# Down product of a conv-FFN: tokens in the partitions, 512 weight columns at a time

## The chip, the cores and the metric

One core of a Trainium2 chip runs the whole layer as one program. The metric is the device time of one execution in microseconds; before the change it is the median of 3 runs.

## What is computed

One layer of a hybrid backbone over 256 latent tokens with 2048 channels. The change lies in its last step, the gated MLP with its residual. Cut to that:

```python
def conv_ffn(h, w_up, conv_w, conv_b, w_down):
    u = h @ w_up
...
    gate, val = jnp.split(u, 2, axis=-1)
    return (jax.nn.silu(gate) * val) @ w_down
...
    x_new = x + g1 * mix_l
    h2_l = modulate(rms_norm(x_new, norm2_w), sh2, sc2)
    x_new = x_new + g2 * conv_ffn(h2_l, w_up, conv_w, conv_b, w_down)
```

`w_down` is 5632 x 2048 in float32, `g2` is one factor per channel (2048 of them), and the first `x_new`, called `x1` in the kernel, is added at the end.

## The kernel before

All activations stand with channels in the 128 partitions and tokens in the free dimension: `x1` is 16 tiles of 128 channels x 256 tokens, the gated MLP's inner values are 44 tiles `g[j]` of 128 x 2 x 256. Products are made in float32r from split operands: a value is a rounded high part and the remaining low part, and a product is high x high, low x high and high x low. In `g`, index 1 of the middle dimension is the high part of the activations and 0 the low part.

Weights come by SyncE's queue (SP) through `fetch` (L225, L227) into four buffers `wraw` of 128 x 1024 (512 KB each). `split` (L201) makes of 512 columns a high part `whi` on ScalarE (ACT, a cast, L206) and a low part `wlo` by a subtraction (L213) on VectorE (DVE), or, if `splits[1]` is not 0, every so many times on GpSimd (POOL). `whi` and `wlo` have four buffers each, so a cast waits until TensorE (PE) has done with the `whi` of four casts before.

The MLP's up stage (L1236 to L1246) works a tile of 128 gate and one of 128 value columns at a time, in two of the four `acc` banks of PSUM. `added` (L272) takes a bank out: a copy on ACT (L273), then an addition on DVE (L274). Convolution and SiLU follow on ACT and DVE (L1211 to L1222), and the result is split into `g[j]` (L231, L232). Between these, the vector of modulation factors is made up: DVE takes products of `w_ada` rows with the conditioning row `cb` (L338, one for each 128 x 1024 block that `araw` holds); `ada_done(48)` at L1247 finishes the last 16 columns of `adav`, which are `g2` (columns 48 to 63) by channel.

The down stage (L1248 to L1254) loops over the 16 tiles `c` of 128 output channels. For each, `col_tile` (L238) streams the 44 weight tiles of 128 x 128: the weights are loaded into the array, and `g` streams past. The high weights take 512 columns (both parts of 256 tokens, L262), the low weights 256 (L264), so a tile is 44 pairs. Then two DVE operations (L1252, L1253) add both halves of the bank, scaled by `adav`, to `x1[c]`, and ACT issues a store of 128 x 256 (L1254). The output leaves transposed and is turned on the host side.

What sets the order: PE's instructions of the stage are tied in the order of the code by `chain`. On the other engines a list scheduler orders the instructions by its own estimate of times, and each engine then executes its list strictly in that order; a waiting instruction holds all behind it. DMAs wait on the queue of the engine that issues them. The framework gives every DMA of SP and ACT one of eight semaphores in turn, in the order of its list (DMAHW0 to DMAHW7 in the rows below); a DMA waits until the earlier DMA on its semaphore has landed, unless that is known already.

## Time and profile before

| | us |
|---|---|
| median of 3 runs | 1700.16 (1699.24 to 1700.27) |
| profiled execution | 1700.9 |
| its span | 1699.1 |
| down stage, first to last start of its matmuls | 1450.0 to 1695.1 |
| PE busy in the span | 1680.0 |
| DVE, ACT busy in the span | 1241.0, 980.0 |

The page and the views show one execution, the profiled one; its own time is 1.8 us longer than its span. Busy time of an engine counts no waiting, no register and no DMA-issuing instructions. Matmuls are pipelined: a row of the timeline can say that a matmul lasts 0.39 us while the next starts 0.23 us later, so PE's pace is read from the starts. A row of a group gives line, engine, operation, output<-inputs, shape and count, then busy us and mean ns of one, then the idle time just ahead of it and what ended that. ACTq and SPq are the queues of ACT and SP in which DMAs are issued.

### The profile page before, as it was taken

Reading aid. Unit: us, or ns where it says so; the run is one execution under the profiler, and the core shown is the slowest. Engines: PE = TensorE matmul, PEld = TensorE weight load, DVE = VectorE, ACT = ScalarE, POOL = GpSimd, SP = SyncE. Lnnn points to the kernel's source line nnn. Section 1 sums busy time; section 2 is a strip of 40 time slices with the busy share of each in tenths; the row PEclk is TensorE's granted clock in tenths of the full one; section 3 lists DMA queues with packets and bytes.
Section 4 is the critical chain, followed back from the end, with each engine's and each line's share of the span. In section 5 each row is a group of like instructions: output and inputs, shape, how many; then the busy total and the mean of one; then the engine's idle time right before and its main releaser. Section 6 shows DMA issues by size and latency. Waiting matters only on the chain.

```text
span 1699.1 us, 29122 instructions
## 1 busy us (share of the span) xinstructions
PE 1680.0 (99%) x10460; PEld 1461.7 (86%) x10460; DVE 1241.0 (73%) x2375; ACT 980.0 (58%) x1984; POOL 310.9 (18%) x331
## 2 busy tenths in 40 slices
PE   7999999999999999999999999999999999999999
PEld 5779999998787888888888998888888888888887
DVE  5556765867688888788988797787878787644443
ACT  5324554756355777666766686666666666444443
POOL 0000213131210000001323200222222222222222
PEclk9999999999999999999999999999999999999999
DMA  9995532434566555688777566676767676666664
GB/s 384 402 408 194 165 127 90 140 109 155 181 200 233 172 188 186 203 280 279 267 260 261 181 200 217 217 238 224 237 227 237 222 241 223 199 203 193 199 201 135
DMA packets 108451, 368.75 MB, mean 217 GB/s; under 512 B 12176, under 2 KB 17040, under 8 KB 108304
## 3 DMA queue, kind: packets, MB, share of 16 engines
q1 hardware_dynamic: 103264, 362.51, 64.0%
q10 hardware_dynamic: 5040, 4.37, 0.8%
q8 instruction: 82, 1.34, 0.3%
q14 instruction: 65, 0.53, 0.1%
HBM read 364.73 MB, written 2.10 MB: 216 GB/s over the span
## 4 chain that ended last, share of the span: by engine, by line
PE 91%; DMA 4%; DVE 3%; ACT 1%; issue 1%; POOL 0%; SPq 0%; DVEq 0%; ACTq 0%
PE down L262 9%; PE upg L262 9%; PE upv L262 9%; PE gate L262 7%; PE down L264 5%; PE upg L264 5%; PE sweep L350 5%; PE upv L264 4%; PE gate L264 4%; PE mix L262 4%; PE mix L264 2%; PE pgb L262 2%; PE ab L350 2%; PE pga L262 2%; DMA ada<-in_w_ad 2%; PE dk L313 2%
## 5 line engine op out<-in xcount | busy, mean ns | idle before, releaser
L206 ACT CAST whi<-wraw 128x512 fp32r<-128x512 f32 (+2 forms) x1004 | 606.5, 608 | 397.3 <-PE down L262 110.5
L213 DVE TENSOR_TENSOR wlo<-wraw,whi 128x512 fp32r<-128x512 f32 (+2 forms) x888 | 608.6, 694 | 251.9 <-ACT whi L206 242.1
L213 POOL TENSOR_TENSOR wlo<-wraw,whi 128x512 fp32r<-128x512 f32 x116 | 157.0, 1353 | 576.4 <-ACT whi L206 555.5
L262 PE MATMUL down<-g,whi 128*128 128x512 f32 x704 | 243.6, 392 | 0.0
L262 PE MATMUL upg<-a,whi 128*128 128x512 f32 x656 | 229.0, 391 | 0.0
L262 PE MATMUL upv<-a,whi 128*128 128x512 f32 x656 | 229.0, 391 | 0.0
L264 PE MATMUL down<-g,wlo 128*128 128x256 f32 x704 | 195.4, 280 | 0.7 <-DVE wlo L213 0.7
L264 PE MATMUL upv<-a,wlo 128*128 128x256 f32 x656 | 182.8, 280 | 0.0
L264 PE MATMUL upg<-a,wlo 128*128 128x256 f32 x656 | 182.6, 280 | 0.0
L262 PE MATMUL gate<-a,whi 128*128 128x512 f32 x512 | 180.5, 398 | 0.7 <-ACT whi L206 0.7
L338 DVE CUSTOM_DVE_ANT_0 araw<-araw,cb 128x1024 f32<-128x1024 f32 x128 | 159.5, 1248 | 11.4 <-DMA araw<-in_w_ada 11.3
L262 PEld LDWEIGHTS down<-g,whi 128*128 128x128 f32 x704 | 131.0, 187 | 28.3
L262 PEld LDWEIGHTS upv<-a,whi 128*128 128x128 f32 x656 | 122.4, 187 | 26.6
L262 PEld LDWEIGHTS upg<-a,whi 128*128 128x128 f32 x656 | 122.4, 187 | 26.5
L264 PE MATMUL gate<-a,wlo 128*128 128x256 f32 x512 | 140.4, 284 | 0.0
L264 PEld LDWEIGHTS down<-g,wlo 128*128 128x128 f32 x704 | 132.9, 189 | 1.9 <-DVE wlo L213 1.0
L264 PEld LDWEIGHTS upv<-a,wlo 128*128 128x128 f32 x656 | 123.9, 189 | 0.5
L264 PEld LDWEIGHTS upg<-a,wlo 128*128 128x128 f32 x656 | 123.9, 189 | 0.5
L262 PEld LDWEIGHTS gate<-a,whi 128*128 128x128 f32 x512 | 94.4, 188 | 20.5 <-ACT whi L206 1.0
L264 PEld LDWEIGHTS gate<-a,wlo 128*128 128x128 f32 x512 | 96.5, 189 | 6.2 <-issue 1.8
L262 PE MATMUL mix<-a,whi 128*128 128x512 f32 x256 | 88.8, 396 | 0.0
L264 PE MATMUL mix<-a,wlo 128*128 128x256 f32 x256 | 69.0, 280 | 0.0
(343 smaller groups left out, 3324.9 us busy)
## 6 DMA issues: line engine op xcount, KB each, us to landing
wraw<-in_w_up SPq DMA_DIRECT2D x164, 512.0 KB, 4.3
araw<-in_w_ada SPq DMA_DIRECT2D x128, 512.0 KB, 4.9
wraw<-in_w_down SPq DMA_DIRECT2D x80, 512.0 KB, 3.9
ada<-in_w_ad SPq DMA_DIRECT2D x64, 512.0 KB, 10.0
wraw<-in_w_gate SPq DMA_DIRECT2D x64, 512.0 KB, 4.3
wraw<-in_w_in SPq DMA_DIRECT2D x58, 512.0 KB, 4.2
wraw<-in_w_proj SPq DMA_DIRECT2D x32, 512.0 KB, 4.3
wraw<-in_w_out SPq DMA_DIRECT2D x32, 512.0 KB, 4.6
```

Source lines behind the costliest of these rows:

```text
L206: copied[0] = S.copy(hi[:, :n], raw)
L213: i = e.tensor_tensor(lo[:, :n], raw, hi[:, :n].bitcast(F32), op=ALU.subtract)
L262: i = PE.matmul(b.rearrange("p (a b) -> p a b", a=2), whi[:, sl], acts[k], start=first, stop=last)
L264: i = PE.matmul(b[:, T:], wlo[:, sl], acts[k][:, 1, :], start=False, stop=last)
L313: PE.matmul(o, whi[:, sl], hi[k], start=first and j == 0, stop=False)
L338: i = V.tensor_tensor_reduce(raw, raw, cb[:, q * 1024:(q + 1) * 1024], 1.0, 0.0, op0=ALU.mult, op1=ALU.add, accum_out=ada2[:, j, q:q + 1])
L350: return kept(PE.matmul(*args, **kw))
```

## The change

The down product is turned: the activations `g` are loaded into the array (128 tokens at a time), and the weights stream past, 512 columns at a time. The output then has its tokens in the partitions and its channels in the free dimension. It is worked in two halves `h` of 1024 channels; each half has four banks (two blocks of 128 tokens, two blocks of 512 channels) that are all open over the whole loop `k` of 44 weight rows. One fetch brings the 128 x 1024 weights of a `k`, two splits make 2 x 512 of it, and each split feeds six matmuls of 512 columns. In the second half the last two `k` are done bank after bank. All low parts are made by DVE (`splits[1] = 0`).

Since the output is turned, the gate and `x1` have to be, too. `residual(k)`, called after each `k` of the first half, does it. The gate: DVE transposes 32 x 32 blocks of `adav` into `gt` (L1281), 2 x 16 transfers on ACT's queue bring its rows into four partitions of `line` (L1261), which POOL has zeroed (L1256), and a shuffle on DVE spreads them into `cb` (L1262). `x1`: DVE transposes its 32 x 32 blocks into `turned` (L1269, four per group `m`), and 32 transfers per group on ACT's queue put the blocks into `row` (L1275), 32 partitions x 4 x 32 each; four groups, 128 transfers. `done` (L1314 to L1316) multiplies a bank by `cb`, adds `row` and stores 128 x 512; the last bank goes in two pieces of 256 columns.

```diff
--- before.py
+++ after.py
@@ -102,7 +102,7 @@
     first = np.concatenate([w_up[:, s:s + P] for s in order[:UPS]], axis=1)
     a["w_up0"] = np.ascontiguousarray(first.reshape(KT, P, UPS * P))
     a["w_up"] = _tiles(w_up, order[UPS:])
-    a["w_down"] = _tiles(np.asarray(i["w_down"])[0], range(0, D, P))
+    a["w_down"] = np.ascontiguousarray(np.asarray(i["w_down"])[0].reshape(FT, P, 2, 1024).transpose(2, 0, 1, 3))
     wf, wb = np.asarray(i["w_a_up_f"])[0], np.asarray(i["w_a_up_b"])[0]
     wa = np.zeros((32, NPAIR, 2, P), wf.dtype)
     wa[:RANK, :, 0] = wf.reshape(RANK, NPAIR, P)
@@ -1245,13 +1245,98 @@
                     splits[1] = PSH2
                     ada_next(32 / (FT - CONVS))
             ada_done(48)
-            for c in range(KT):
-                b = acc_bank("down")
-                col_tile(I["w_down"][c], gs, b, orders(c, FT // 4, 0, 2))
-                y = temp()
-                V.scalar_tensor_tensor(y, b[:, :T], adav[:, 48 + c:49 + c], x1[c], op0=ALU.mult, op1=ALU.add)
-                V.scalar_tensor_tensor(y, b[:, T:], adav[:, 48 + c:49 + c], y, op0=ALU.mult, op1=ALU.add)
-                nc.scalar.dma_start(out[c * P:(c + 1) * P, :], y)
+
+            splits[1] = 0
+            gt = pf.tile([P, 32], F32, name="gt")
+            rows = []
+
+            def gate_line(h):
+
+                line = st.tile([P, 1024], F32, tag="araw", bufs=2, name="line")
+                G.memset(line, 0.0)
+                for r in range(0, P, 32):
+                    to = line[r:r + 1, :].rearrange("o (c p j) -> o c p j", c=8, p=4)
+                    for p in range(4):
+                        o = 32 * p + 16 + 8 * h
+                        nc.scalar.dma_start(to[:, :, p, :], gt[o:o + 8, :])
+                return lambda: V.stream_shuffle(cb[:, 1024 * h:1024 * (h + 1)], line, [0] * 32)
+
+            def turn(m):
+
+                rows.append([hp.tile([P, 512], F32, tag=f"a{4 * t + m}", name="row") for t in range(2)])
+                turned = st.tile([P, 1024], F32, tag="araw", bufs=2, name="turned").rearrange("p (c t) -> p c t", c=4)
+                for c in range(4):
+                    V.transpose(turned[:, c, :], x1[4 * m + c])
+                return turned
+
+            def move(m, turned, p):
+                for q in range(8):
+                    to = rows[m][q // 4].rearrange("p (c n) -> p c n", c=4)
+                    nc.scalar.dma_start(to[32 * (q % 4):32 * (q % 4 + 1), :, 32 * p:32 * (p + 1)],
+                                        turned[32 * p:32 * (p + 1), :, 32 * q:32 * (q + 1)])
+
+            def residual(k):
+
+                if k == 2:
+                    V.transpose(gt, adav[:, 32:64])
+                elif k in (3, 4):
+                    ready.append(gate_line(k - 3))
+                elif k in (6, 7):
+                    ready.pop(0)()
+                elif 8 <= k < 28:
+                    m, p = divmod(k - 8, 5)
+                    if p == 0:
+                        ready[:] = [turn(m)]
+                    else:
+                        move(m, ready[0], p - 1)
+
+            ready = []
+
+            def pieces(k):
+
+                raw = fetch(I["w_down"][h, k], 1024)
+                return [split(raw[:, n * 512:(n + 1) * 512], 512) for n in range(2)]
+
+            def part(t, n, k, w):
+                ts = slice(t * P, (t + 1) * P)
+                g = gs[k]
+                for a, b in ((1, 0), (0, 0), (1, 1)):
+                    i = PE.matmul(banks[t][n], g[:, a, ts], w[n][b], start=k == 0 and (a, b) == (1, 0),
+                                  stop=k == FT - 1 and b == 1)
+                    if chain:
+                        after(i, chain[0])
+                    chain[:] = [i]
+
+            def done(t, n, cols=slice(0, 512)):
+
+                o = slice(1024 * h + 512 * n + cols.start, 1024 * h + 512 * n + cols.stop)
+                y = hp.tile([P, 512], F32, tag=f"a{8 + 4 * h + 2 * t + n}", name="y")[:, :cols.stop - cols.start]
+                V.tensor_tensor(y, banks[t][n][:, cols], cb[:, o], op=ALU.mult)
+                V.tensor_tensor(y, y, rows[2 * h + n][t][:, cols], op=ALU.add)
+                nc.scalar.dma_start(out[t * P:(t + 1) * P, o], y)
+
+            for h in range(2):
+                banks = [[acc_bank("down") if h == 0 else aux_bank("down", t) for n in range(2)] for t in range(2)]
+                last = FT - 2 if h else FT
+                for k in range(last):
+                    w = pieces(k)
+                    for n in range(2):
+                        for t in range(2):
+                            part(t, n, k, w)
+                    if h == 0:
+                        residual(k)
+                if h == 0:
+                    for t in range(2):
+                        for n in range(2):
+                            done(t, n)
+
+            ws = [pieces(k) for k in range(last, FT)]
+            for n in range(2):
+                for t in range(2):
+                    for k in range(last, FT):
+                        part(t, n, k, ws[k - last])
+                    for cols in [slice(0, 512)] if not (n and t) else [slice(0, 256), slice(256, 512)]:
+                        done(t, n, cols)
 
 
 def kernel(**inputs):
@@ -1262,9 +1347,8 @@
     arrays = _lay_out(inputs)
     I = {n: nc.dram_tensor(f"in_{n}", a.shape, mybir.dt.from_np(a.dtype), kind="ExternalInput").ap()
          for n, a in arrays.items()}
-    out = nc.dram_tensor("out_yt", (D, T), F32, kind="ExternalOutput").ap()
+    out = nc.dram_tensor("out_y", (T, D), F32, kind="ExternalOutput").ap()
     with tile.TileContext(nc, schedule_with_timeline_sim=True) as tc:
         layer_kernel(tc, I, out)
     r = _run(nc, [{f"in_{n}": a for n, a in arrays.items()}], core_ids=[0])
-    yt = np.asarray(r.results[0]["out_yt"])
-    return np.ascontiguousarray(yt.T).reshape(1, T, D)
+    return np.asarray(r.results[0]["out_y"]).reshape(1, T, D)
```

How the lists change. First ACT, at the start of the down stage. Before, the casts of weights (L206) follow each other with the last up tile's work (L1211, L1221, L231: convolution, SiLU, split of `g[43]`) between them:

```order
L273 COPY C_7758<-upv 128x256
L206 CAST whi<-wraw 128x512
L1221 ACTIVATE C_7960<-C_7960 128x256
L1211 ACTIVATE C_6178<-C_7758,vec 128x256
L206 CAST whi<-wraw 128x512 x2
L231 CAST g_16646<-C_7960 128x256
L206 CAST whi<-wraw 128x512 x9
L1254 DMA out_yt<-C_6289 128x256
```

In the change, from the cast for `k` = 3's second half (the one after the second single line transfer) on:

```order
L206 CAST whi<-wraw 128x512
L1261 DMA line<-gt 1x8x32 x12
L206 CAST whi<-wraw 128x512 x2
L1261 DMA line<-gt 1x8x32 x16
L206 CAST whi<-wraw 128x512 x4
L1275 DMA row<-turned 32x4x32 x5
```

The 32 transfers of the gate that the code spreads over two steps stand in two runs of 12 and 16 here, with two casts between them. Later on ACT, a block of eight moves of `x1` between pairs of casts, with the semaphores that each waits for:

```order
L206 CAST whi<-wraw 128x512 [waits DVE_49,PE_49] x2
L1275 DMA row<-turned 32x4x32 [waits DMAHW4_49]
L1275 DMA row<-turned 32x4x32 [waits DMAHW5_49]
L1275 DMA row<-turned 32x4x32 [waits DMAHW6_49]
L1275 DMA row<-turned 32x4x32 [waits DMAHW0_49]
L1275 DMA row<-turned 32x4x32 [waits DMAHW1_49]
L1275 DMA row<-turned 32x4x32 [waits DMAHW2_49]
L1275 DMA row<-turned 32x4x32 [waits DMAHW3_49]
L1275 DMA row<-turned 32x4x32 [waits DMAHW4_49]
```

The fifth of these follows a load of weights on its semaphore (that for `k` = 18), the others follow moves. In nearly every block one move, often the third, waits so for a load that SP issued shortly before. There are thirteen such blocks, up to the casts for `k` = 28; four casts stand together after the first, fifth and ninth of them, else two.

On DVE, at the start of the stage. Before:

```order
L338 ISA araw,ada_77<-araw,cb 128x1024
L338 ISA ada_77 128x1
L213 TENSOR_TENSOR wlo<-wraw,whi 128x512
L1214 SCALAR_TENSOR_TENSOR C_7960<-C_7556,vec,C_7960 128x255
L672 TENSOR_TENSOR adav<-ada_77 128x16
L274 TENSOR_TENSOR C_7758<-upv,C_7758 128x256
```

In the change, the same place:

```order
L338 ISA araw,ada_77<-araw,cb 128x1024
L338 ISA ada_77 128x1
L213 TENSOR_TENSOR wlo<-wraw,whi 128x512
L1214 SCALAR_TENSOR_TENSOR C_7960<-C_7556,vec,C_7960 128x255
L672 TENSOR_TENSOR adav<-ada_77 128x16
L213 TENSOR_TENSOR wlo<-wraw,whi 128x512
L274 TENSOR_TENSOR C_7758<-upv,C_7758 128x256
```

A subtraction (L213) now stands ahead of the addition that empties the last up tile's bank (L274). Further on there, the new operations stand ahead of subtractions, too:

```order
L213 TENSOR_TENSOR wlo<-wraw,whi 128x512 x2
L1262 STREAM_SHUFFLE cb<-line 128x1024
L213 TENSOR_TENSOR wlo<-wraw,whi 128x512
L1269 STREAM_TRANSPOSE turned<-C_6178 128x256
L1269 STREAM_TRANSPOSE turned<-C_6289 128x256
L1269 STREAM_TRANSPOSE turned<-C_6569 128x256
L1269 STREAM_TRANSPOSE turned<-C_6846 128x256
L213 TENSOR_TENSOR wlo<-wraw,whi 128x512
L1262 STREAM_SHUFFLE cb<-line 128x1024
```

The subtraction between shuffle and transposes is that for the second half of `k` = 4, the one ahead of the second shuffle that for the first half of `k` = 5. The two pieces of the last bank take the same buffer `y` (`done` asks for it by its tag), so the second piece's multiplication waits on the first piece's store.

## The prediction, made before the change was run

> **What bounds the kernel now.** I read the page's first part, then the view of the tile `down`, then the stretch that holds the down product, then single instructions. The page says that TensorE (PE) is busy nearly all the time.
>
> ```profile
> span 1699.1 us, 29122 instructions
> PE 1680.0 (99%) x10460; PEld 1461.7 (86%) x10460; DVE 1241.0 (73%) x2375; ACT 980.0 (58%) x1984; POOL 310.9 (18%) x331
> ```
>
> The view of `down` gives count, durations (min/median/max in ns) and first and last start; the stretch view gives the stretch, its length, busy time and count of PE, PEld, DVE, ACT and POOL, the granted clock, and the DMA engines' share and rate.
>
> ```profile
> L262 PE MATMUL down<-g,whi x704: 390/391/403, 1450.0 to 1694.9; 128*128 128x512 f32 x176
> L264 PE MATMUL down<-g,wlo x704: 274/280/384, 1450.4 to 1695.1; 128*128 128x256 f32 x176
> 1450.00:1695.00 245.00, 244.31 (x1409) 214.81 (x1408) 108.53 (x171) 108.82 (x177) 56.82 (x44) 1.00 0.63 190
> ```
>
> The product lasts 245.1 us from first to last start, PE is without a gap in it (244.31 of 245.00), DVE and ACT are under half busy. So the stage is PE's own, and what counts is PE's pitch and whether anything makes it wait. In the timeline (start, duration) the starts give the pitch:
>
> ```profile
> 1499.69 0.39 PE L262 MATMUL down<-g,whi 128*128 128x512 f32 x1
> 1499.92 0.28 PE L264 MATMUL down<-g,wlo 128*128 128x256 f32 x1
> 1500.04 0.39 PE L262 MATMUL down<-g,whi 128*128 128x512 f32 x1
> ```
>
> A pair of 512 and 256 columns takes about 0.35 us (245.1 / 704 = 0.348).
>
> **The change part by part. The product itself.** Three matmuls of 512 columns replace two pairs: 1056 matmuls for 704 pairs, the same columns. The dv projection already has this form, activations loaded and 512 weight columns streamed:
>
> ```profile
> 429.84 0.39 PE L277 MATMUL dvb<-whi,a 128*128 128x512 f32 x1
> 430.07 0.39 PE L278 MATMUL dvb<-whi,a 128*128 128x512 f32 x1
> ...
> 432.56 0.39 PE L277 MATMUL dvb<-whi,a 128*128 128x512 f32 x1
> ```
>
> Twelve starts in 2.72 us: 0.2267 us each. 1056 x 0.2267 = 239.4 us, so the term is **-5.7 us**. The Trainium skill ("TensorE: Matmul & The Clock Gate", Back-to-back issue gap) puts a warm matmul of N columns at N/2.4 + 2.5 ns, an estimate of 216 ns here. By it the sum would be 11.5 us lower; the trace's 227 ns for this very form decides.
>
> **The first banks.** The stage now opens four banks at once, and the tenth matmul (due 9 x 0.2267 = 2.0 us after the first) writes the bank of the last up tile, which DVE's L274 must have read.
>
> ```profile
> 1450.91 2.25 DVE L338 CUSTOM_DVE_ANT_0 araw<-araw,cb 128x1024 f32<-128x1024 f32 x1 [0.77 <-DMA araw<-in_w_ada]
> ...
> 1454.18 0.41 DVE L274 TENSOR_TENSOR C<-upv,C 128x256 f32<-128x256 f32 x1
> L338 DVE CUSTOM_DVE_ANT_0 araw<-araw,cb 128x1024 f32<-128x1024 f32 x128 | 159.5, 1248 | 11.4 <-DMA araw<-in_w_ada 11.3
> L213 DVE TENSOR_TENSOR wlo<-wraw,whi 128x512 fp32r<-128x512 f32 x244 | 168.8, 692 | 150.0 <-ACT whi L206 149.4 <-PE upv L264 0.5
> ```
>
> L274 ended 4.6 us after the first down matmul; nobody needed it then. The new order puts one more subtraction (0.69) before it: 5.3 - 2.0 = **+3.2 us** (2.2 if L338 takes its mean of 1.25, 4.2 if yet another second is lost).
>
> **The transfers on ACT.** ACT gets 32 gate lines and 128 moves between the casts that feed PE. What one costs ACT, and how long one takes to land:
>
> ```profile
> 0.71 0.41 ACTq L354 DMA_DIRECT2D ccol<-in_ccol  x1
> 1.15 0.45 ACTq L355 DMA_DIRECT2D ident<-in_ident  x1
> ...
> 1467.65 0.62 ACT L206 CAST whi<-wraw 128x512 fp32r<-128x512 f32 x1 [0.71 <-PE down L262]
> 1467.67 0.35 ACTq L1254 DMA_DIRECT2D out_yt<-C  x1
> L1254 ACTq DMA_DIRECT2D out_yt<-C x16: 338/338/353, 1467.7 to 1696.5; - x16
> wraw<-in_w_down SPq DMA_DIRECT2D x80, 512.0 KB, 3.9
> xr<-in_xl ACTq DMA_DIRECT2D x16, 128.0 KB, 5.1
> out_yt<-C ACTq DMA_DIRECT2D x16, 128.0 KB, 3.3
> wr<-in_w_a SPq DMA_DIRECT2D x4, 96.0 KB, 2.0
> ```
>
> An issue holds ACT's queue 0.34 us, with 0.03 to the next issue (0.71 + 0.41 to 1.15): 0.37. It runs beside a cast already started (1467.65 and 1467.67), but a cast behind it waits. Total, 160 x 0.37 = 59 us beside some 120 us of the first half: room enough on average. But the order bunches them, and each DMA waits until the earlier one on its semaphore, of eight, has landed; a weight load is often that one (3.9 us). The small ones' landing isn't in the trace: the nearest rows say 2.0 (96 KB) to 5.1; I take 2.5, near the smallest.
>
> *Gate lines.* Call C0, C1, ... the casts of the stage, two per k; PE spends 6 x 0.2267 = 1.36 us on each. Four buffers let C7 start when PE has done with C3: 5.2 + 3.2 = 8.4 us after the first matmul. Behind C7 stand twelve lines; the eleventh waits for the weight load that DVE's subtraction for C7 frees: 8.4 + 0.62 + 0.69 + 1.1 for two operations ahead of it on DVE (0.41 and 0.69) = 10.8, landed 14.7. Two more issues, then C8 is done at 16.0 (due 8 x 1.36 + 3.2 = 14.1). Behind C9 stand sixteen more. The thirteenth waits for a load that waits for the subtraction for C9, which stands behind the shuffle, which waits for the first lines to land.
>
> ```profile
> L643 DVE STREAM_SHUFFLE rt<-nraw 128x256 f32<-128x256 f32 x16 | 7.1, 444 | 0.0
> L206 ACT CAST whi<-wraw 128x512 fp32r<-128x512 f32 x324 | 200.7, 620 | 179.1 <-PE down L262 110.5 <-PE upg L262 36.7 <-PE down L264 12.6
> ```
>
> Lines landed 17.6; shuffle at four times 0.444 = 1.78 to 19.4; subtraction 20.1; load landed 24.0; four issues 1.5 and the cast: C10 done at 26.1, due 16.8: 9.3 late. The second shuffle holds the subtraction for C11 the same way: last line landed 27.6, subtraction done 30.1, wanted 27.9: 2.2. Together **+11.5 us** (8 with landings of 2.0 and a shuffle of 1.2, 17 with landings of 5.1).
>
> *Moves.* The first 24 stand one or two behind a cast: hidden. From there, thirteen blocks of eight. The chain for two k: cast 0.62, subtraction 0.69, load 3.9, the third move of a later block that waits for it and the five behind it 6 x 0.37 = 2.2, dispatch 0.2: 7.6, so 3.8 per k against PE's 12 x 0.2267 = 2.72. Thirteen blocks x 1.08 = 14.0, less some 3.0 of head start in the four buffers. Twice DVE's transposes (4 x 0.44, by the shuffle's row) stand ahead of a subtraction and wait for a block to land; that is 2.5 + 1.8 after the block's last issue where 1.3 (cast and subtraction) would do, 3.0 late, and about half shows past the head start: 3.0 for both. **+14.0 us** (0 if the chain is under 5.4 per two k, 36 if a landing takes 5.1, since then a lane comes round only every 5.5 us: 13 x 2.75).
>
> *Clock.* A wait of some us slows PE afterwards:
>
> ```profile
> 462.00:464.00 2.00, 0.62 (x3) 0.58 (x4) 1.59 (x5) 1.59 (x5) 0.00 (x0) 1.00 0.29 119
> 464.00:466.00 2.00, 2.00 (x7) 1.66 (x7) 1.82 (x7) 0.35 (x1) 0.00 (x0) 0.50 0.04 8
> ```
>
> PE idle for most of 2 us, then a granted clock of 0.50 for about 3.4 us: 1.7 lost. The wait before C10 is 5 us long; part of the loss hides under the wait that follows: **+1.0 us** (0 to 3.4).
>
> **What costs nothing.** The subtractions that POOL did return to DVE: 176 x 0.69 = 122 us of 240, no bound. POOL's two memsets of `line` fall on an engine that is then idle. The operations L1252 and L1253 and the stores that go away lay beside PE's work, all but the last of each, which the end counts. Between the halves eight DVE operations of some 0.69 mix with four subtractions: the first can start 0.85 us after PE begins k = 43, so the last subtraction is done at 0.85 + 12 x 0.69 = 9.1 and wanted at 7 x 1.36 + 0.45 = 10.0. That cover hides them; 1 to 2 us without it.
>
> **The end.**
>
> ```profile
> 1695.10 0.28 PE L264 MATMUL down<-g,wlo 128*128 128x256 f32 x1
> 1695.41 0.48 DVE L1252 SCALAR_TENSOR_TENSOR C<-down,adav,C 128x256 f32<-128x256 f32 x1 [5.71 <-PE down L264]
> 1695.93 0.48 DVE L1253 SCALAR_TENSOR_TENSOR C<-down,adav,C 128x256 f32<-128x256 f32 x1
> 1696.45 0.34 ACTq L1254 DMA_DIRECT2D out_yt<-C  x1
> ```
>
> Now 4.0 us lie between the last start and the end: 0.31, two operations 1.04, the store 2.65. The change ends in two halves of 256 columns that share one buffer, so the second half's first operation waits until the first store has landed: 0.31 + 1.04 + 2.65 + 1.04 + 2.65 = 7.7: **+3.7 us** (+2.7 with a quicker store).
>
> **Sum**: -5.7 + 3.2 + 11.5 + 14.0 + 1.0 + 3.7 = +27.7. The profiled execution took 1700.9 us (1.8 around its span), 0.7 above the median of the runs: 1728.6 on its scale, 1728 against the median.
>
> **The rivals.** *Issues that cost ACT nothing.* For it: the store's issue ran inside a cast. Against: 0.44 between issues at the start. Then the move chain is 5.2 per two k, below 5.44, and no block is late; the gate lines keep their landings (C8 1.2 late, C10 7.4 in all, the next subtraction 2.6): -5.7 + 3.2 + 10.0 + 1.0 for the transposes + 1.0 + 3.7 = +13.2, so 1713. The Trainium skill ("DMA: Bandwidth & Descriptors", Issuing engines are not separate DMA queues) says that starting a DMA costs the sequencer little beside the DMA itself. The trace speaks against it here, with 338 ns per issue.
>
> *Slow landings*, 5.1 like `xr`. For it speaks the load on the DMA engines (the row gives packets, MB and share of 16 engines):
>
> ```profile
> q10 hardware_dynamic: 5040, 4.37, 0.8%
> ```
>
> ACT's packets took 0.008 x 16 x 1699 / 5040 = 43 ns each, at 870 bytes. The moves are 128 x 128 = 16384 packets of 128 bytes; at the same 43 ns, which bounds them from above, that is 44 us of each engine inside some 70 us, on top of a share of 0.63. Against it: smaller packets should take less. Gate 17, moves 36: -5.7 + 3.2 + 17 + 36 + 1.0 + 3.7 = +55, so 1755.
>
> *Everything hides.* For it: ACT and DVE are under half busy, and the casts run four buffers ahead. The deciding place is C10: from C7 at 8.4 to 16.2 there are 7.8 us for 28 lines, so an issue must cost under 0.28 us and no landing may be waited for. Then -5.7 + 3.2 + 3.7 = +1.2, so 1701; and -5.7, 1694, if the first banks and the end hide too.
>
> **How the numbers follow.** Forecast 0.64, issues free 0.18, slow landings 0.08, everything hides 0.10, half of it on either side of no change. About 0.2% (3.4 us) is what a measurement can tell. So faster 0.05, same 0.05, slower 0.90. The range leaves out the last two and the tails: 1709 (issues free with quick landings) to 1745 (landings about 4).
>
> **What would show it.** Right: PE starts 0.227 us apart in the second half and 239 us in all without the waits; a PE gap of about 3 us near the tenth down matmul behind L274; gaps of about 5 us behind casts and about 2 behind subtractions in the first 35 us; ACT's rows full of DMA issues with a cast only every 3.8 us per pair until about k = 28; 7.7 us behind the last matmul. Wrong: no PE gaps in the first half (the last rival), an issue well under 0.3 us, or small landings far from 2.5 us.

## The result and the profile after

The changed kernel takes 1743.54 us (median of 5, 1741.70 to 1746.26) against 1700.16 us: a ratio of 1.0262, with a 95% interval of 1.0249 to 1.0274 (the two medians alone give 1.0255). The forecast was 1728, with a range of 1709 to 1745. It is slower, as forecast, by 43 us where the forecast had 28. The profiled execution of the changed kernel took 1743.49 us. One execution of an experiment below, of the first one with the moves from HBM, took 2770 us at a granted clock of 0.56 and is left out of its median.

The page's first part and the row of the granted clock (one digit for a fortieth of the span, 43.5 us):

```profile
span 1741.6 us, 28584 instructions
...
PE 1692.5 (97%) x10108; PEld 1450.4 (83%) x10108; DVE 1271.8 (73%) x2426; ACT 977.8 (56%) x1984; POOL 251.7 (14%) x289
...
PEclk9999999999999999999999999999999998989999
```

The span is 42.5 us longer. PE is busy 12.5 us longer, though it has fewer matmuls (10108 for 10460), and its clock drops in two slices of the down stage. The view of the tile `down` (count, duration min/median/max in ns, first and last start):

```profile
L1304 PE MATMUL down<-whi,g x704: 387/389/796, 1448.8 to 1734.2; 128*128 128x512 f32 x176
...
L1304 PE MATMUL down<-wlo,g x352: 387/389/796, 1449.3 to 1734.4; 128*128 128x512 f32 x176
```

The first and the last start are 285.6 us apart where it was 245.1 (+40.5); 7.2 us lie behind the last start (+3.2); the stage begins 1.2 us earlier. That is the 42.5. The median matmul is as short as it should be (389 ns), the longest twice as long (796): look for waits and for a halved clock. First the stretches of the stage (length, PE's busy time and count, granted clock, share of the DMA engines, GB/s), then what PE waited for in the stage (us, times, longest):

```profile
1450.00:1475.00 25.00, 15.70 (x56) 0.85 0.32 104
1475.00:1500.00 25.00, 23.78 (x94) 0.87 0.65 177
1500.00:1525.00 25.00, 17.80 (x63) 0.93 0.54 138
1525.00:1550.00 25.00, 19.68 (x64) 0.85 0.48 128
1550.00:1575.00 25.00, 21.04 (x73) 0.87 0.54 147
1575.00:1600.00 25.00, 25.00 (x112) 1.00 0.67 209
1615.00:1734.00 119.00, 119.00 (x527) 1.00 0.56 188
```

```profile
PE down L1304 <- ACT whi L206: 25.5, 12, 5.4
PE down L1304 <- DVE C L274: 1.2, 1, 1.2
PE down L1304 <- DVE wlo L213: 0.4, 1, 0.4
```

All of the loss lies in the first 125 us, where the small transfers are; from 1575 on there is no gap. PE waited 25.5 us for ACT's casts. By an estimate from these rows, busy time at a clock under 1 adds 15.70 x 0.15 + 23.78 x 0.13 + 17.80 x 0.07 + 19.68 x 0.15 + 21.04 x 0.13 = 12.4 us. Against an even pitch of 0.2267 us the matmuls are 46.0 us late at 1571, and 46.4 from 1572 on. Of this the tenth matmul is 1.4, waits on ACT and DVE are 25.9, the clock some 12.4; the other 6 or 7 us lie in the matmuls right behind a wait, which start 0.34 to 0.39 us behind their forerunner.

What ACT did instead of casting is in the rows of its transfers (duration min/median/max in ns) and in its timeline (start, duration):

```profile
L1261 ACTq DMA_DIRECT2D line<-gt x32: 627/627/1272, 1453.1 to 1474.8; - x32
```

```profile
L1275 ACTq DMA_DIRECT2D row<-turned x128: 592/612/987, 1475.9 to 1569.6; - x128
```

```profile
1456.58 7.97 ACTq L1261 DMA_DIRECT2D line<-gt  x12
...
1465.48 9.98 ACTq L1261 DMA_DIRECT2D line<-gt  x15
1475.55 0.62 ACT L206 CAST whi<-wraw 128x512 fp32r<-128x512 f32 x1 [9.77 <-DMA line<-gt]
...
1507.81 5.85 ACTq L1275 DMA_DIRECT2D row<-turned  x7
1513.76 0.62 ACT L206 CAST whi<-wraw 128x512 fp32r<-128x512 f32 x1 [5.54 <-DMA row<-turned]
1513.87 0.59 ACTq L1275 DMA_DIRECT2D row<-turned  x1
1514.28 0.62 ACT L206 CAST whi<-wraw 128x512 fp32r<-128x512 f32 x1
1514.50 4.55 ACTq L1275 DMA_DIRECT2D row<-turned  x7
1519.14 0.62 ACT L206 CAST whi<-wraw 128x512 fp32r<-128x512 f32 x1 [4.24 <-DMA row<-turned]
...
1530.78 6.19 ACTq L1275 DMA_DIRECT2D row<-turned  x7
```

An issue of these transfers takes ACT's sequencer 0.61 to 0.63 us, not the 0.34 of a store; with the step to the next it is 7.97 / 12 = 0.66 for a line and 4.55 / 7 = 0.65 for a move. Two casts with a list of eight (in the rows the first of the eight issues starts before the second cast does) come round after 1519.14 - 1513.76 = 5.38 us. What PE makes of two casts is one step of the inner dimension, and it takes 12 x 0.2267 = 2.72 us for it. Two of the thirteen lists took over 1 us longer, the rows of 5.85 and 6.19 for seven moves: in each, one move was issued 1.4 us late, when a load of weights by SP, the earlier DMA on its semaphore, had landed.

The end, where the two halves of the last bank share a buffer:

```profile
1734.40 0.39 PE L1304 MATMUL down<-wlo,g 128*128 128x512 f32 x1
1734.82 0.42 DVE L1314 TENSOR_TENSOR y<-down,cb 128x256 f32<-128x256 f32 x1
...
1737.75 0.42 DVE L1314 TENSOR_TENSOR y<-down,cb 128x256 f32<-128x256 f32 x1 [2.04 <-DMA out_y<-y]
```

### The profile page after: what moved, and what is told of

It is laid out like the page before. It is cut to its first block, busy times and chain, and to the rows that moved or that the text cites. A ratio compares the mean times of both kernels' runs of the same rounds, so it can differ in the third digit from the quotient of the medians.

```text
span 1741.6 us, 28584 instructions
## 1 busy us (share of the span) xinstructions
PE 1692.5 (97%) x10108; PEld 1450.4 (83%) x10108; DVE 1271.8 (73%) x2426; ACT 977.8 (56%) x1984; POOL 251.7 (14%) x289
## 3 DMA queue, kind: packets, MB, share of 16 engines
q10 hardware_dynamic: 22976, 6.51, 1.6%
## 4 chain that ended last, share of the span: by engine, by line
PE 87%; DMA 5%; DVE 4%; ACTq 2%; ACT 1%; issue 1%; DVEq 0%
PE down L1304 10%; PE upg L262 9%; PE upv L262 9%; PE gate L262 7%; PE sweep L350 5%; PE upg L264 4%; PE upv L264 4%; PE gate L264 4%; PE mix L262 3%; DMA row<-turned 2%; PE ab L350 2%; PE mix L264 2%; PE pgb L262 2%; PE pga L262 2%; PE dk L313 2%; PE dk L315 2%
## 5 line engine op out<-in xcount | busy, mean ns | idle before, releaser
L206 ACT CAST whi<-wraw 128x512 fp32r<-128x512 f32 (+2 forms) x1004 | 604.5, 608 | 443.3 <-DVE wlo L213 87.9
L213 DVE TENSOR_TENSOR wlo<-wraw,whi 128x512 fp32r<-128x512 f32 (+2 forms) x932 | 636.1, 693 | 278.4 <-ACT whi L206 266.0
L1304 PE MATMUL down<-whi,g 128*128 128x512 f32 x704 | 227.5, 406 | 26.6 <-ACT whi L206 25.5
L1304 PEld LDWEIGHTS down<-whi,g 128*128 128x128 f32 x704 | 136.8, 196 | 60.7 <-ACT whi L206 31.2
L338 DVE CUSTOM_DVE_ANT_0 araw<-araw,cb 128x1024 f32<-128x1024 f32 x128 | 160.1, 1252 | 11.5 <-DMA araw<-in_w_ada 11.4
L213 POOL TENSOR_TENSOR wlo<-wraw,whi 128x512 fp32r<-128x512 f32 x72 | 100.1, 1390 | 388.3 <-ACT whi L206 371.4
L1304 PE MATMUL down<-wlo,g 128*128 128x512 f32 x352 | 143.2, 407 | 0.4 <-DVE wlo L213 0.4
L1304 PEld LDWEIGHTS down<-wlo,g 128*128 128x128 f32 x352 | 69.1, 196 | 20.0 <-DVE wlo L213 5.6
```

What stands on the lines that cost most here:

```text
L206: copied[0] = S.copy(hi[:, :n], raw)
L213: i = e.tensor_tensor(lo[:, :n], raw, hi[:, :n].bitcast(F32), op=ALU.subtract)
L338: i = V.tensor_tensor_reduce(raw, raw, cb[:, q * 1024:(q + 1) * 1024], 1.0, 0.0, op0=ALU.mult, op1=ALU.add, accum_out=ada2[:, j, q:q + 1])
L1304: i = PE.matmul(banks[t][n], g[:, a, ts], w[n][b], start=k == 0 and (a, b) == (1, 0), stop=k == FT - 1 and b == 1)
```

## The experiments

Two theories stood after this. One: ACT's sequencer is held 0.65 us by each transfer, and the lists stand between the casts, so ACT's own queue sets the pace (and behind waits of some us the clock is halved). The other is the prediction's: the landings of weights and of small transfers, on which a queued DMA waits, set it. The kernel before ran beside every experiment; its median there was 1699.6 to 1700.0.

### The product alone, and each list alone

Without the lines and the moves (leaves out the gate and the residual):

```
-                    V.transpose(gt, adav[:, 32:64])
-                elif k in (3, 4):
-                    ready.append(gate_line(k - 3))
...
-                        move(m, ready[0], p - 1)
+                    G.memset(cb, 1.0)
...
+                        G.memset(rows[m][t], 0.0)
```

> The product in its new form alone: no transfer for the gate and none for x1 (the gate is set to 1 and the residual rows to 0 by fills, so this kernel leaves out the gate and the residual). Theory 1 (the whole loss of the changed kernel is in its 160 small transfers on ACT's queue): the last matmul of the changed kernel started 46.0 us later than a gap-free stream would have, 1.4 of it at the tenth matmul; the other 44.6 go, so 1743.5 - 44.6 = 1699, within 2 us. Theory 2 (part of the loss belongs to the product itself: 512 columns of weights at a time split on two engines, fed by fewer and wider loads): some of the 44.6 us stays, 1705 to 1720, with waits on the casts left in the trace.

Measured: 1699.35 us, ratio 0.9997 (0.9987 to 1.0006). The matmuls of this kernel in the view of `down`:

```profile
L1299 PE MATMUL down<-whi,g x704: 387/390/494, 1449.6 to 1690.2; 128*128 128x512 f32 x176
...
L1299 PE MATMUL down<-wlo,g x352: 388/390/398, 1450.0 to 1690.4; 128*128 128x512 f32 x176
```

The stage takes 240.8 us; only the tenth matmul waits. So the product in its new form loses nothing, and the whole 44.2 us between 1699.35 and 1743.54 belong to the gate lines and the moves with what they need.

Without the lines, with the moves (leaves out the gate):

```
-                    V.transpose(gt, adav[:, 32:64])
-                elif k in (3, 4):
-                    ready.append(gate_line(k - 3))
-                elif k in (6, 7):
-                    ready.pop(0)()
+                    pass
+                elif k == 3:
+                    G.memset(cb, 1.0)
```

> The gate's 32 line transfers, its two fills and two shuffles are left out (the gate is set to 1, so this kernel leaves out the gate); the 128 moves of x1 stay. Theory 1 (each small transfer holds ACT about 0.65 us, and each list of eight costs by itself): the moves' share stays as it was, 29.7 us above the product alone, 1728 within 4 us. Theory 2 (the lines' 15 us of delay left the weights without a lead, and the moves only cost so much because of that): the moves cost what the prediction gave them, 14 us, so about 1713.

Measured: 1723.23 us, ratio 1.0138 (1.0123 to 1.0153): 23.9 us for the moves, between the two. Without the lines the scheduler also puts the moves in another order: 48 of them stand one to three behind a cast, and then come ten lists of eight, where the changed kernel has 24 and thirteen lists. The 48 cost 0.5 us (the matmuls were 2.0 us late after the first bank and 2.5 at 1498.28, ahead of the first list's effect); the ten lists cost 22.0 (24.5 late at the last start). In the changed kernel the same ten lists (from those behind C32 and C33 on, as the prediction counts the casts) cost 22.4 (24.1 late at 1518.91, 46.4 at the end), and the moves ahead of them, three lists among them, 7.8 (24.1 less the 16.3 that the lines and the first bank had cost). So the lists have their own price, with or without the lines, and the lines add to it by the three more lists. The moves' landings, in the DMA view's column at the end, were 3.1 us:

```profile
row<-turned ACTq DMA_DIRECT2D x128, 16.0 KB, 3.1
```

With the lines, without the moves and their transposes (leaves out the residual):

```
                     if p == 0:
-                        ready[:] = [turn(m)]
-                    else:
-                        move(m, ready[0], p - 1)
+                        rows.append([hp.tile([P, 512], F32, tag=f"a{4 * t + m}", name="row") for t in range(2)])
+                        for t in range(2):
+                            G.memset(rows[m][t], 0.0)
```

> The counterpart to the run without the lines: the gate's 32 line transfers stay on ACT's queue, the 128 moves of x1 and their transposes are left out (the residual rows are filled with 0, so this kernel leaves out the residual). Theory 1 (the lines hold ACT 20.8 us in two lists, at a time when few weights are ahead, and each list also leaves the matmuls at half rate for about 3 us): the lateness at the twelfth cast in the changed kernel was 16.3 us, of which 1.4 is the first bank, so 1699.4 + 14.9 = 1714, within 2 us. Theory 2 (the two parts do not add: without the moves behind it the stage catches up, or without the lines the moves were cheaper than their place suggests, 23.9 us measured for 29.7): the lines' share is 44.2 - 23.9 = 20.3 us by difference, 1719.7.

Measured: 1714.33 us, ratio 1.0085 (1.0071 to 1.0099), so 15.0 us for the lines, as their place in the changed kernel said (14.9). With 15.0 and 23.9 the lines and the moves cost 38.9 alone and 44.2 together. The 5.3 between them stand where the changed kernel has its three more lists; whether a lead lost to the lines has a part in it was not taken apart.

### The price of an issue

The moves read from x in HBM, in their shape, not tied to the transposes:

```
-                                        turned[32 * p:32 * (p + 1), :, 32 * q:32 * (q + 1)])
+                                        I["xl"][32 * p:32 * (p + 1), 4 * m:4 * m + 4, 32 * q:32 * (q + 1)])
```

> The 128 moves keep their shape and their place on ACT's queue but read from the input x in HBM and not from the turned tile in SBUF (this changes what is added: x untransposed for x1). Nothing has to be waited for then, so they also start earlier and stand two at a time between the casts. Theory 1 (the issue is long because source and target are both in SBUF): the issue falls from 0.61 to about 0.34 us, as at the loads of weights and the stores, ACT is freed of 128 x 0.27 = 35 us, and the time is 1712 to 1722, of which 15 us belong to the lines that stay. Theory 2 (the issue is long because of the many small pieces, whatever the source): it stays at 0.6 us, and the time is above 1725, less only what the better spreading saves.

Measured: 1722.06 us, ratio 1.0129 (1.0112 to 1.0146). The same moves, tied behind the transposes, so that the last ten lists of eight (the expectation counts nine) stand between the same casts as in the changed kernel:

```
-                for c in range(4):
-                    V.transpose(turned[:, c, :], x1[4 * m + c])
-                return turned
+                return [V.transpose(turned[:, c, :], x1[4 * m + c]) for c in range(4)][-1]
...
+                    after(nc.scalar.dma_start(to[32 * (q % 4):32 * (q % 4 + 1), :, 32 * p:32 * (p + 1)],
+                                              I["xl"][32 * p:32 * (p + 1), 4 * m:4 * m + 4, 32 * q:32 * (q + 1)]), turned)
```

> The 128 moves read from the input x in HBM as in the earlier run, but each is tied behind the transposes, so that nine lists of eight stand between the same casts as in the changed kernel and the rest two or three at a time (this changes what is added: x untransposed for x1). Theory 1 (the length of an issue decides, and the chain that the prediction worked out for a list of eight is right once its price is): at 0.32 to 0.44 us for an issue a list of eight holds ACT 2.8 to 3.7 us, the moves cost 8 to 16 us in place of 29.7, and the time is 1722 to 1730. Theory 2 (the lists cost by their place, whatever an issue takes): 1738 to 1744.

Measured: 1725.67 us, ratio 1.0154 (1.0138 to 1.0169). The issues and one list of this kernel:

```profile
L1273 ACTq DMA_DIRECT2D row<-in_xl x128: 317/442/1670, 1475.4 to 1551.3; - x128
```

```profile
1511.11 0.62 ACT L206 CAST whi<-wraw 128x512 fp32r<-128x512 f32 x1 [2.92 <-DMA row<-in_xl]
...
1511.73 3.34 ACTq L1273 DMA_DIRECT2D row<-in_xl  x7
1515.16 0.62 ACT L206 CAST whi<-wraw 128x512 fp32r<-128x512 f32 x1 [2.91 <-PE down L1302]
```

The same shape, target and place, another source: the median issue falls from 612 to 442 ns, the round of a list (two casts and eight issues) from 5.38 to 1515.16 - 1511.11 = 4.05 us. Against PE's 2.72 that is 1.33 over where it was 2.66, half the excess. The ten lists cost half, too: 11.7 us (16.9 late at 1511.03, 28.6 at the last start) where they cost 22.4. (Two of these rounds took 6.8 and 5.6 us; in them, moves waited for loads of weights on their semaphores.) All moves cost 1725.67 - 1714.33 = 11.3 us where they cost 29.2 (1743.54 - 1714.33), but of these 29.2 some 7.8 stood ahead of the ten lists, where this kernel has three lists fewer. The clock is whole over all of the lists, and most waits there are under 1.2 us:

```profile
1482.00:1575.00 93.00, 85.79 (x360) 1.00 0.64 192
```

This is the run that shows the issue's length as the cause. The first of the two runs agrees (its moves cost 7.7 us over the lines) but stands at the upper end of its expectation: its issue is 0.44, neither the 0.34 of one theory nor the 0.6 of the other. So the source is not all: a load from HBM without these pieces of 128 bytes took 344 ns (that of `row`, in the kernel by way of HBM below).

### Another queue, or other spacing

All 160 on POOL's queue, nothing left out (both `nc.scalar.dma_start` in `gate_line` and `move` become `nc.gpsimd.dma_start`):

```
-                        nc.scalar.dma_start(to[:, :, p, :], gt[o:o + 8, :])
+                        nc.gpsimd.dma_start(to[:, :, p, :], gt[o:o + 8, :])
```

> All 160 small transfers go out on POOL's queue; nothing is left out. Theory 1 (they cost because they hold ACT between the casts): the waits on the casts by ACT go, and what is left are the tenth matmul and the end: 1699 to 1705. Theory 2 (they cost by their traffic or by their landings, on whichever queue they stand: the weights' transfers share the DMA engines with them): the time stays within 10 us of the changed kernel, 1733 to 1745. If POOL issues them no faster than 1.2 us each, the 160 take 190 us and still fit into the stage, but the row for the second half of the columns may come late.

Measured: 1700.19 us, ratio 1.0003 (0.9993 to 1.0013). The moves' issues, and their landings, in this kernel:

```profile
L1275 POOL DMA_DIRECT2D row<-turned x128: 548/548/598, 1474.9 to 1579.7; - x128
...
DMA to landing us min/median/max: 1.7/3.6/6.9
```

An issue nearly as long (548 ns) and landings no quicker (3.6 us), and PE waits for nothing but the first bank: long issues and slow landings cost nothing on a queue that no cast stands in. But more than the queue changed. In the view of the DMA queues (packets, MB, share of 16 engines) the 160 transfers are 5120 packets on POOL's queue (q0), where they were 22976 - 4032 = 18944 on ACT's (q10; 4032 are its other transfers); and on POOL's queue they have semaphores of their own, so that none waits for a load of weights. First the changed kernel, then this one:

```profile
q10 hardware_dynamic: 22976, 6.51, 1.6%
...
q0 software_dynamic: 5120, 2.14, 0.6%
```

So this run alone does not refute the traffic; the next one, with ACT's queue and the same 18944 packets, does. The Trainium skill ("DMA: Bandwidth & Descriptors", Issuing engines are not separate DMA queues) says that starting DMAs on several engines at once saves only the time that it takes the sequencer to start them, which is usually small beside the DMA itself. Here it is small beside a landing of 3.1 us (0.61), so the trace agrees, though the prediction read it the other way; but 160 of them ahead of casts were worth 43 us.

The same transfers on ACT's queue, four for each step:

```
+                if 2 <= k < 10:
+                    for _ in range(4):
+                        lines[(k - 2) // 4][0].pop(0)()
...
+                if 10 <= k < 42:
+                    m, i = divmod(k - 10, 8)
+                    for q in range(4):
+                        move(m, moves[m], i // 2, i % 2 * 4 + q)
```

> The same 160 transfers on the same queue of ACT, four for each step of the inner dimension: the lines in steps 2 to 9, the moves in steps 10 to 41; nothing is left out. A step takes the matmuls 12 x 0.2267 = 2.72 us, and ACT 4 x 0.65 + two casts. Theory 1 (bunching: eight or sixteen issues in a row hold the casts longer than the lead of the weights): the waits fall from 45 to under 15 us, 1700 to 1713. Theory 2 (not the bunches but ACT's total in the stage counts, which is 160 x 0.65 = 104 us beside its casts): with four per step ACT is a little slower than the matmuls, so about 0.3 to 0.6 us are lost in each of 40 steps, 1712 to 1725. Theory 3 (landings, whatever the order): 1733 to 1745.

Measured: 1706.98 us, ratio 1.0038 (1.0026 to 1.0049). One stretch over the stage's first 150 us, and PE's waits in this kernel:

```profile
1450.00:1600.00 150.00, 144.45 (x619) 1.00 0.67 205
```

```profile
PE down L1308 <- DVE wlo L213: 3.3, 4, 1.4
PE down L1308 <- DVE C L274: 1.8, 1, 1.8
```

The issues are as many and as long as in the changed kernel (median 612 and 627 ns), in the same packets, and 7.6 us are lost against the product alone in place of 44.2 (the matmuls are 9.8 late at the end, 2.0 of it at the first bank). Four issues, 2.6 us, fit into a step of 2.72 us; no wait of PE is over 1.8 us, the longest being that for the first bank, and the clock stays at 1.00. So neither the traffic nor the total of ACT's time was the price, but the lists were.

### By way of HBM

The gate and x1 turned through a scratch tensor in HBM, 77 transfers in place of 160, nothing left out:

```
+            def store(m, turned, p, c):
+                nc.scalar.dma_start(xd[m].rearrange("(q a) c n -> a c q n", a=32)[:, c, :, 32 * p:32 * (p + 1)],
+                                    turned[32 * p:32 * (p + 1), c, :].rearrange("a (q n) -> a q n", q=8))
...
+                    for p in range(4):
+                        nc.scalar.dma_start(gd[:, p, :], gt[32 * p + 16:32 * p + 32, :])
...
+                    nc.scalar.dma_start(cb, gd.rearrange("c p n -> (c p n)").rearrange("(o n) -> o n", o=1).to_broadcast([P, D]))
...
+                            nc.scalar.dma_start(rows[m][t], xd[m][t * P:(t + 1) * P].rearrange("a c n -> a (c n)"))
```

> The gate and x1 are turned round by way of HBM, on ACT's queue as before and with nothing left out: 4 stores and one load broadcast over the partitions for the gate (no fills, no shuffles), 64 stores of 32x8x32 and 8 loads of 128x512 for x1, 77 transfers in place of 160. Theory 1 (the price is ACT's time in issues, and a transfer with one end in HBM is issued in 0.34 us): 77 x 0.37 = 28 us of issues in place of 104, in groups of four, 1.5 us each, so that the waits on the casts fall to under 5 us: 1700 to 1706. Theory 2 (the issue takes 0.63 us whatever its ends): 50 us of issues, groups of 2.6 us, waits of 10 to 20 us: 1710 to 1720.

Measured: 1706.53 us, ratio 1.0035 (1.0022 to 1.0048); 7 us above the product alone, a little more than expected. The stores' issues took 461 ns in the median, and a few far more (1338 at most). A stretch and two rows of ACT in this kernel:

```profile
1475.00:1500.00 25.00, 24.32 (x95) 16.33 (x93) 12.29 (x20) 9.31 (x16) 0.00 (x0) 1.00 0.90 236
```

```profile
1468.81 3.99 ACTq L1264 DMA_DIRECT2D xd<-turned  x2
1472.89 0.62 ACT L206 CAST whi<-wraw 128x512 fp32r<-128x512 f32 x1 [3.49 <-DMA cb<-gd]
```

Two issues held ACT 3.99 us: the second stood until the broadcast of the gate, the earlier DMA on its semaphore, had landed, 7.9 us after its issue. So here a landing did cost, by the wait that the prediction had expected of the moves. The DMA engines are at 0.90 in this stretch (0.65 in the same one after the change). What of the 7 us is this, and what the issues, was not taken apart.

### The end and the first bank

One result tile for both halves of the last bank:

```
+                if (h, t, n) not in ys:
+                    ys[h, t, n] = hp.tile([P, 512], F32, tag=f"a{8 + 4 * h + 2 * t + n}", name="y")
+                y = ys[h, t, n][:, cols]
```

> One change to the changed kernel: the two halves of the last bank share one result tile and write to their own columns of it, so that the second half no longer waits until the first half's store has landed. Theory 1 (the end is 7.2 us for that wait of 2.04 us and the store behind it, against 4.0 before): the end falls by 2 to 3 us, 1740.5 to 1741.5, and the row of the wait on the store is gone. Theory 2 (the end is set by the latency of the last store alone, and the wait lies beside it): within 0.5 us of the changed kernel, 1743.

Measured: 1741.72 us, ratio to before 1.0244 (1.0229 to 1.0260). The wait on the store is gone from the view; 5.0 us lie behind the last matmul's start in place of 7.2. The medians give 1.8 us, a little less than the 2 to 3 expected. Together with the way through HBM:

> The turn by way of HBM together with one result tile for the two halves of the last bank; nothing is left out. If both gains hold and add, 2 to 3 us less than the turn by way of HBM alone: 1697 to 1703, that is not slower than the kernel before its change and perhaps 0.2 percent faster. If the theory on the issues falls, 1707 to 1717.

Measured: 1703.66 us, ratio 1.0019 (1.0010 to 1.0028), 2.9 less than without, though still above before and 0.7 above the expected range. With the transfers on POOL instead:

> All 160 small transfers on POOL's queue and one result tile for the two halves of the last bank; nothing is left out. The transfers on POOL gave 1700.2 us, and the shared result tile took 1.8 us off the changed kernel. If both add: 1698.4, a ratio of 0.999 to the kernel before. If the end is not shortened here, because the other stores on ACT's queue now stand closer: 1700.

Measured: 1697.89 us, ratio 0.9991 (0.9982 to 1.0000): as added up, but the interval touches no change. Then also the fourth bank from the other set:

```
-                banks = [[acc_bank("down") if h == 0 else aux_bank("down", t) for n in range(2)] for t in range(2)]
+                banks = [[(acc_bank("down") if (t + n == 2) == (h > 0) else aux_bank("down", t)) for n in range(2)] for t in range(2)]
```

> The same, and in the first half of the columns the fourth bank is one of those that the second half uses (and the other way round), so that the tenth matmul no longer waits for the subtraction out of the last up tile; nothing is left out. If the wait of 1.15 to 1.8 us goes and nothing takes its place: 1.2 to 1.6 us less than without this, about 1697, a ratio of 0.998. If the weights behind it are as late as that bank: no difference.

Measured: 1696.38 us, ratio 0.9977 (0.9967 to 0.9987), so 0.23% faster than the kernel before the change. Its stage:

```profile
L1304 PE MATMUL down<-whi,g x704: 387/389/397, 1448.1 to 1687.0; 128*128 128x512 f32 x176
...
L1304 PE MATMUL down<-wlo,g x352: 388/389/397, 1448.5 to 1687.2; 128*128 128x512 f32 x176
```

239.1 us from the first to the last start, 1055 steps of 0.2267: the stage without a wait, as long as the prediction's first term had it.

## Why the prediction was right or wrong

- **The product, -5.7.** Right. The last kernel above has the 239 us of the working, by the pitch of the dv projection (0.2267) and not by the estimate of 216 ns that stood beside it.
- **The first bank, +3.2.** Right in kind, 1.4 in size. The matmul and what it waited for:

```profile
1452.22 0.73 PE L1304 MATMUL down<-whi,g 128*128 128x512 f32 x2 [1.15 <-DVE C L274]
```

```profile
1448.92 1.22 DVE L338 CUSTOM_DVE_ANT_0 araw<-araw,cb 128x1024 f32<-128x1024 f32 x1
...
1451.75 0.41 DVE L274 TENSOR_TENSOR C<-upv,C 128x256 f32<-128x256 f32 x1
```

The operation L338 ahead of it took 1.22 us, not the 2.25 of before, and began 0.1 us after the stage's first matmul, not 0.95. Its length before was an exception, and what made it so is not shown: POOL was subtracting beside it, but most others with POOL beside them took 1.22, too. The lower bound given, 2.2 with L338 at its mean, was the better value.
- **The gate lines and the clock, +11.5 and +1.0.** The sum was near (12.5 for 15.0), its parts were not. The working had issues of 0.37 and two waits on a weight load of 3.9 each. The trace has no such wait: the median line takes 627 ns, as the shortest does. What the 28 issues cost more, 28 x (0.66 - 0.37) = 8.1, stands where 7.8 of landings were put. So C8 and C10, worked out for 16.0 and 26.1 us after the first matmul, opened the way for PE at 16.5 and 27.4. The 2.2 for the second shuffle did not come: PE waited 0.4 us for DVE's low parts in the whole stage. Two errors cancelled, so the near sum is luck; the rows of the stores gave no hint of it.
- **The moves, +14.0.** Here the forecast failed in size: 29.2 to 30.1 for 14.0 (by the medians, and by the lateness behind the lines). The step is "with 0.03 to the next issue (0.71 + 0.41 to 1.15): 0.37": it took the price of loads and stores with one end in HBM for transfers from SBUF to SBUF in pieces of 128 bytes, which take 0.65. By it a list of eight was 3.8 us a step, with a landing of 3.9 in the chain. In the trace it is 5.38, with no landing waited for in most lists, and 6.7 and 7.0 in the two with a wait for a load. The chain named the wrong limiter too: in most lists ACT's own queue, 8 x 0.65 and two casts partly beside it, sets the round. The 3.0 for the transposes did not come either. With HBM as the source, at 0.44 an issue, the moves cost 11.3 in all and the ten lists half of what they had cost, which shows that the price was what was off; that 11.3 is near the 14.0 shows little, since three lists fewer stood there.
- **The clock, +1.0 with at most 3.4.** Put beside the gate alone, and too small. It came behind later waits as well, some 12.4 us in all; but a step at half rate, with starts 0.43 us apart, takes 12 x 0.43 = 5.2 us, less than the 5.38 of a round, so part of it only shortens the waits that follow. Behind the lines' two waits it was 3.98 x 0.50 + 5.18 x 0.49 = 4.5:

```profile
1465.30:1469.30 4.00, 3.98 (x9) 0.50 0.06 12
1476.20:1481.40 5.20, 5.18 (x12) 0.51 0.40 109
```

- **The end, +3.7.** Right: 3.2, for the named wait.
- **The rivals.** "Issues that cost ACT nothing" is refuted by the rows above. "Slow landings" is refuted by the run on POOL, where the moves land in 3.6 us and nothing waits, and by the four for each step; where a landing was measured on ACT's queue, it was 3.1 us, not 2.5. "Everything hides", at 1701, described what happens once the issues leave ACT: 1700.2. Its turning point, an issue under 0.28 us, is beside the point there: the issue still took 0.55, but no cast stood behind it.

By the traces the terms are -5.7 + 1.4 + 14.9 + 29.7 (46.0 - 16.3) + 3.2, less the 1.2 by which the stage begins earlier: +42.3, for the 42.5 between the spans. The forecast's 27.7 lacked the 15.7 of the moves above all. The result lies inside the range, 1.5 us below its upper end; but that end was put there for landings of about 4 us, and that issues nearly twice as long came out below it is luck.

## What to carry to other kernels

Price a DMA on a compute engine's queue by a row with the same two ends and the same pieces (SBUF to SBUF is not HBM to SBUF), and multiply by the longest list between two instructions that feed the bottleneck, not by the total. A list has to fit into the time the bottleneck needs for what that engine feeds it; if it doesn't, spread it or put it on a queue that nobody waits for. The product here only paid (0.23%) when the transfers, the end and the first bank were all taken off PE's path.

## What the runs showed of the hardware

An issue on ACT's queue took 338 ns for a store of SBUF to HBM (256 or 128 KB), 344 ns for HBM to SBUF (256 KB), 442 ns in the median for HBM to SBUF in pieces of 128 bytes, 612 to 627 ns for SBUF to SBUF, with no more for 16 KB than for 1 KB. On POOL's queue the same SBUF to SBUF transfers took 518 to 551 ns, in about a quarter of the packets.

A wait of 2.1 us was enough for half rate, though not each time: in all the profiled executions thirteen waits of the down stage were 2.0 to 2.4 us long, and eleven of them were followed by it. One wait of the changed kernel with the stretch behind it, then one of the kernel with the moves from HBM in the old order:

```profile
1525.19 0.85 PE L1304 MATMUL down<-whi,g 128*128 128x512 f32 x2 [2.09 <-ACT whi L206]
```

```profile
1525.20:1529.20 4.00, 4.00 (x10) 0.57 0.23 32
```

```profile
1526.67 0.73 PE L1302 MATMUL down<-whi,g 128*128 128x512 f32 x2 [2.11 <-ACT whi L206]
```

```profile
1526.60:1528.60 2.00, 1.93 (x7) 1.00 0.23 34
```

The shortest wait that half rate followed is one that all fourteen kernels have far ahead of the stage, in five of them; here in the kernel before, ahead of the stretch of 464 to 466 us that the prediction shows:

```profile
463.38 0.50 PE L262 MATMUL dq<-a,whi 128*128 128x512 f32 x1 [1.51 <-DVE osq L288]
```

The Trainium skill ("TensorE: Matmul & The Clock Gate", Why this matters for your kernels) tells to avoid idle gaps above some 3 us. In these kernels gaps a third shorter, and one of half that length, could already be followed by a halved clock. Behind the wait of 2.09 us it cost 4.00 x (1 - 0.57) = 1.7 us more, so a gap can cost nearly twice its length.
